# SwiGLU of a decoder block on one Trainium2 core: first products of four weight blocks in a row, scalings moved to VectorE, weight sums later

## The chip, the core and the metric

The kernel runs on one core of a Trainium2 chip. TensorE multiplies, VectorE, ScalarE and GpSimd work on tiles of 128 partitions, and SyncE (SP) issues most of the DMAs. The metric is the device time of one execution in microseconds (us).

## What is computed

A decoder block with one layer: three mixing branches, their gated sum projected and added to `h`, then a SwiGLU, and a last norm. The change lies in the SwiGLU and in what leads into it:

```python
D_MODEL = 1024; SEQ = 1024; N_META = 16; D_FF = 2816

h = h + m @ w_o
hn = rms_norm(h, norm2_g)
gate, up = jnp.split(hn @ w_gate_up, 2, axis=-1)
return h + (jax.nn.silu(gate) * up) @ w_down
# afterwards: rms_norm(h, final_g)[:, N_META:]
```

## The kernel before

Activations lie transposed: features on the partitions, the 1024 tokens along the rows of a tile, in two halves of 512. Full precision is kept by splitting every operand into a high half (fp32r, a cast on ScalarE) and a low half (the rest, a subtraction on VectorE or GpSimd). A product of two operands is three matmuls a slice, high x high, high x low, low x high, in `gemm` (lines 268 to 270). A "product" below is four slices of 128 features with 512 tokens, 12 matmuls.

The projection `w_gate_up` is worked off in 22 blocks of 128 output columns. A block is a 2x2 product: the weights are A11, A12 (the two halves of the gate's 1024 input features) and A21, A22 (the same of the up part); the normed `h` is B11, B21 (first 512 tokens, first and second 512 features) and B12, B22 (the other 512 tokens). It is done with Strassen-Winograd, seven products instead of eight: A11 B11, A12 B21, S1 T1, S4 B22, S2 T2, S3 T3 and A22 T4. S1 to S4 are sums of weights, made on GpSimd for each block (`pair_sums`, lines 1909 to 1912; S1, S2, S4, S3 in this order); T1 to T4 are sums of the B's, made once. `keys` names the B's and T's in the order of the numbers 0 to 6 that `ORDERS` uses. The down projection that follows works in the same manner, in three groups.

Block 0 is written apart in `mlp`: four direct products on B11 and B21 (gate and up), then four on T1 and B22 that add up two and two in PSUM. Blocks 1 to 21 run over `plans` and `steps`: `ahead` makes weight factors (`factor`: cast on ScalarE, low half on VectorE) four products ahead, `gemm` multiplies, and `consume` adds the results up one product later, makes the SiLU, and `put` multiplies gate and up on GpSimd.

The tiles `y{half}{o}` hold `h` for a half of the tokens and eight feature tiles `o`. The first half is normed and split while the output projection runs (`out_proj`, `first`). For the second half `stat(1)` sums squares with TensorE during the first product, `bcast(1)` spreads the factors by TensorE and a ScalarE copy (line 1662), and `sum_t1` scales: tiles 4 to 7 by their gain on ScalarE (`prescale`, line 1717) and by the norm on GpSimd (`scaled_late`, line 1721), tiles 0 to 3 in one instruction on VectorE (`scaled`, line 1712), with T1 (line 1882) behind each. T2 and T4 are made on VectorE (lines 1956, 1957), T3 on GpSimd (line 1955). Low halves have line 295 (`sub_lo`) on every engine, casts of weights line 1782, of the B's and T's line 1796; `halves` puts off each low half until the next cast, and `settle` issues what is left.

Weights come through the tile `raw`: 512 KB for the gate or the up part of a block, two buffers, so a load can only be issued when everything that reads the part two before it is done. SP issues the loads (line 213) in program order. All engines work their queues in the order of the program text; no scheduler moves anything.

Of the kernel before, what the change touches and what calls it, by code (L numbers as in the profile page):

```python
# [123 lines left out]
class Trunk:  # L124
    SLACK = 1500.0

    def __init__(self, tc, a):
# [2175 lines left out]
```

## Time and profile before

| | us |
|---|---|
| median of 3 runs (1750.38 to 1752.44) | 1750.57 |
| the profiled execution | 1750.45 |
| its span, first to last instruction | 1748.7 |
| TensorE busy | 1667.2 (95%) |
| VectorE busy | 1344.6 (77%) |
| ScalarE busy | 763.0 (44%) |
| GpSimd busy | 881.0 (50%) |

Line numbers are those of the kernel before. Times in the views count from the start of the span. `x`, `in<-` and the like read "output <- inputs". An entry in brackets is the time that the engine stood idle before the instruction, and what released it. The stretch of interest begins near 1043 us, where the first product of the SwiGLU starts, and ends near 1105 us, where blocks 0 and 1 are done; the 140 products of the other 20 blocks follow in an unbroken pattern.

### The profile page before, as it was taken

Reading aid. Unit: us, or ns where it says so; the run is one execution under the profiler, and the core shown is the slowest. Engines: PE = TensorE matmul, PEld = TensorE weight load, DVE = VectorE, ACT = ScalarE, POOL = GpSimd, SP = SyncE. Lnnn points to the kernel's source line nnn. Section 1 sums busy time; section 2 is a strip of 40 time slices with the busy share of each in tenths; the row PEclk is TensorE's granted clock in tenths of the full one; section 3 lists DMA queues with packets and bytes.
Section 4 is the critical chain, followed back from the end, with each engine's and each line's share of the span. In section 5 each row is a group of like instructions: output and inputs, shape, how many; then the busy total and the mean of one; then the engine's idle time right before and its main releaser. Section 6 shows DMA issues by size and latency. Waiting matters only on the chain.

```text
span 1748.7 us, 22588 instructions
## 1 busy us (share of the span) xinstructions
PE 1667.2 (95%) x7912; PEld 1383.0 (79%) x7912; DVE 1344.6 (77%) x2100; ACT 763.0 (44%) x1439; POOL 881.0 (50%) x639
## 2 busy tenths in 40 slices
PE   6989999998999999999999998999999999898986
PEld 5778878886888887888778876788888888686866
DVE  7999996588888744888886248777777777979697
ACT  4566217456544444876622234323322324443343
POOL 4322325315555665211174136766666665697664
PEclk9989999999999999999999998999999999999998
DMA  4111123233323333310285431332333226453423
GB/s 148 49 37 33 40 85 108 69 127 101 115 97 112 118 109 119 89 53 1 85 286 184 160 102 38 109 115 91 102 103 126 93 95 233 152 199 121 145 97 115
DMA packets 91922, 190.65 MB, mean 109 GB/s; under 512 B 9552, under 2 KB 21840, under 8 KB 91808
## 3 DMA queue, kind: packets, MB, share of 16 engines
q1 hardware_dynamic: 88704, 184.13, 31.7%
q10 hardware_dynamic: 2992, 4.75, 0.7%
q8 instruction: 62, 1.02, 0.2%
q0 software_dynamic: 112, 0.33, 0.1%
q14 instruction: 52, 0.43, 0.1%
HBM read 135.43 MB, written 53.74 MB: 108 GB/s over the span
## 4 chain that ended last, share of the span: by engine, by line
PE 62%; DVE 7%; DMA 2%; issue 2%; ACT 1%; POOL 1%; DVEq 0%; ACTq 0%; SPq 0%; POOLq 0%
PE ps L268 18%; PE ps L270 18%; PE ps L269 18%; PE ps L1446 2%; DMA y<-T 1%; DVE y L295 1%; PE ps L1422 1%; PE ps L1423 1%; PE ps L1421 1%; PE ps L1470 1%; PE ps L1471 1%; PE ps L1472 1%; DVE y L1712 1%; DVE h L1825 1%; DMA s<-y 1%
## 5 line engine op out<-in xcount | busy, mean ns | idle before, releaser
L268 PE MATMUL ps<-xh,whi 128*128 128x512 f32 (+1 forms) x492 | 175.0, 356 | 4.7 <-DVE u L863 2.4
L270 PE MATMUL ps<-xh,wlo 128*128 128x512 f32 (+1 forms) x492 | 173.9, 354 | 1.1 <-DVE wlo L239 1.1
L269 PE MATMUL ps<-xl,whi 128*128 128x512 f32 (+1 forms) x492 | 174.0, 354 | 0.6 <-POOL xl L295 0.4
L1825 DVE TENSOR_TENSOR c<-c,ps 128x512 f32<-128x512 f32 x175 | 119.4, 682 | 54.3 <-PE ps L270 49.6
L1847 POOL TENSOR_TENSOR h<-c,c 128x512 f32<-128x512 f32 x44 | 68.9, 1585 | 120.8 <-issue 75.1
L1834 ACT ACTIVATE c<-c 128x512 f32<-128x512 f32 x44 | 27.8, 632 | 207.5 <-DVE c L1825 207.5
L268 PEld LDWEIGHTS ps<-xh,whi 128*128 128x128 f32 x492 | 93.6, 190 | 17.8 <-DVE u L863 2.7
L270 PEld LDWEIGHTS ps<-xh,wlo 128*128 128x128 f32 x492 | 93.7, 190 | 14.9 <-DVE wlo L239 1.9
L269 PEld LDWEIGHTS ps<-xl,whi 128*128 128x128 f32 x492 | 93.7, 191 | 13.3 <-POOL xl L295 1.3
L239 POOL TENSOR_TENSOR wlo<-raw,whi 128x1024 fp32r<-128x1024 f32 x21 | 51.7, 2461 | 98.9 <-ACT whi L233 98.9
L269 PE MATMUL ps<-l,whi 128*128 128x512 f32 x232 | 90.9, 392 | 1.3 <-DVE l L295 1.2
L268 PE MATMUL ps<-h,whi 128*128 128x512 f32 x232 | 91.0, 392 | 0.0
L270 PE MATMUL ps<-h,wlo 128*128 128x512 f32 x232 | 90.6, 391 | 0.0
L720 DVE TENSOR_SCALAR_CACHE_REDUCE B<-sc,s 128x912 bf16<-128x912 f32 (+2 forms) x93 | 89.0, 957 | 0.1
L295 DVE TENSOR_TENSOR wlo<-sw,wlo 128x512 fp32r<-128x512 f32 (+1 forms) x49 | 57.1, 1165 | 22.7 <-ACT wlo L1782 19.5
L295 DVE TENSOR_TENSOR op<-raw,op 128x512 fp32r<-128x512 f32 (+1 forms) x42 | 56.3, 1352 | 17.0 <-ACT op L1047 17.0
L295 DVE TENSOR_TENSOR whi<-sw,whi 128x512 fp32r<-128x512 f32 (+1 forms) x50 | 50.6, 1013 | 24.4 <-ACT whi L1782 21.5
L295 DVE TENSOR_TENSOR op<-sw,op 128x512 fp32r<-128x512 f32 (+1 forms) x48 | 52.0, 1088 | 20.1 <-ACT op L1782 19.5
L295 DVE TENSOR_TENSOR whi<-raw,whi 128x512 fp32r<-128x512 f32 (+1 forms) x40 | 53.2, 1331 | 14.2 <-ACT whi L1047 12.7
L2010 POOL TENSOR_TENSOR h<-h,c 128x512 f32<-128x512 f32 x27 | 43.8, 1636 | 31.3 <-DVE c L1825 23.7
L1132 ACT COPY c<-ps 128x512 f32<-128x512 f32 x52 | 30.4, 585 | 63.8 <-PE ps L270 63.7
L1453 POOL CAST pm<-pm 16x512 fp32r<-16x512 f32 x14 | 8.5, 604 | 97.2 <-ACT pm L1449 97.2
(615 smaller groups left out, 5710.8 us busy)
## 6 DMA issues: line engine op xcount, KB each, us to landing
raw<-in_wts_dram SPq DMA_DIRECT2D x136, 512.0 KB, 3.9
T<-h SPq DMA_DIRECT2D x44, 256.0 KB, 5.3
B<-h SPq DMA_DIRECT2D x33, 256.0 KB, 2.0
y<-T SPq DMA_DIRECT2D x33, 256.0 KB, 5.7
y<-b SPq DMA_DIRECT2D x32, 256.0 KB, 2.2
s<-y SPq DMA_DIRECT2D x32, 256.0 KB, 4.9
ga<-c SPq DMA_DIRECT2D x16, 256.0 KB, 3.9
gb<-c SPq DMA_DIRECT2D x16, 256.0 KB, 4.1
```

Of the source, the lines that this page charges most:

```text
L239: e.tensor_tensor(l[:, c], r[:, c], h[:, c].bitcast(F32), op=ALU.subtract)
L268: nc.tensor.matmul(ps[:, :n], wh, xh, start=(start and k == 0), stop=False, **kw)
L269: nc.tensor.matmul(ps[:, :n], wh, xl, start=False, stop=False, **kw)
L270: nc.tensor.matmul(ps[:, :n], wl, xh, start=False, stop=(stop and k == last), **kw)
L295: getattr(self.nc, eng).tensor_tensor(lo, x, hi.bitcast(F32), op=ALU.subtract)
L720: nc.vector.tensor_scalar(junk2[:, :nk_of(i)], self.sc[i], value, None, op0=ALU.is_ge, op1=ALU.add, accum_out=at(cs, i))
L1132: nc.scalar.copy(t, ps)
L1446: nc.tensor.transpose(p3[:rows, h, :], d["S"][h][:, col:col + rows], self.ident)
L1825: nc.vector.tensor_tensor(dst, a, b, op=ALU.add)
L1834: nc.scalar.activation(t, t, AF.Silu)
L1847: nc.gpsimd.tensor_tensor(t, u, s, op=ALU.mult)
L2010: nc.gpsimd.tensor_tensor(a, a, b, op=ALU.add)
```

## The change

For blocks 0 to 3 (`NFIRST`) the two products on the first token half, A11 B11 and A12 B21, come first, eight products in a row (`first`); their results wait in tiles. So only the gate parts are loaded at first, and they are loaded a second time (`regu`) with the up parts, when these blocks run the other five products (`ORDERS[0]`). Block 0 thereby takes seven products as the others do. `prescale` and `scaled_late` go: all eight tiles of the second half are scaled by one VectorE instruction each. T1, B22, T2, T3 and T4 are made piecewise at slices of these products. The weight sums of block 0 are made behind block 3's first product, and its S4 behind block 3's second.

```diff
-ORDERS = ((0, 1, 2, 3, 4, 5, 6), (0, 1, 6, 2, 3, 4, 5), (0, 2, 3, 4, 5))
+ORDERS = ((2, 3, 4, 5, 6), (0, 1, 6, 2, 3, 4, 5), (0, 2, 3, 4, 5))
+NFIRST = 4
...
+    for f in range(NFIRST):
+        units.append(("gu", f * P, KT))
     for f in range(NFF):
-        units.append(("gu", f * P, KT))
+        units.append(("gu" if f >= NFIRST else "regu", f * P, KT))
         units.append(("gu", DFF + f * P, KT))
...
-        def prescale(o):
-            h2 = self.y[o, 1]
-            nc.scalar.activation(h2, h2, AF.Copy, scale=self.cols["g2"][:, o:o + 1])
-
-        def scaled_late(o, eng="gpsimd"):
-            h2 = self.y[o, 1]
-            getattr(nc, eng).tensor_tensor(h2, h2, rbs[1], op=ALU.mult)
-            return h2
...
-        A.append(self.factor(g[:, 512:], "gpsimd"))
+        A.append(self.factor(first_gates[0][:, 512:], "gpsimd"))
+        self.fetch(self.n_get + 2)
         block(w7, 7, 1)
-        A += [self.factor(x, "gpsimd") for x in (u[:, :512], u[:, 512:])]
+        A += [self.factor(first_gates[1][:, q * 512:(q + 1) * 512], "vector") for q in range(2)]
         self.fetch(self.n_get + 3)
...
+    def first_gate(self, f):
+        self.fetch(self.n_get + f)
+        return self.raw.pop(self.n_get + f)
...
-        p1 = self.gemm(A11, X["B11"], 512, {3: stat1})
-        p1s = copied(p1)
-
-        def sum_t1():
-            self.bcast(1)
-            for k in range(4):
-                self.prescale(4 + k)
-            for k in range(4):
-                self.scaled_late(4 + k)
-            for k in range(4):
-                b12 = self.scaled(k, 1)
-                t1 = y[k, 0]
-                nc.vector.tensor_tensor(t1, b12, t1, op=ALU.subtract)
-                self.halves("T1", t1)
-            self.settle()
-
-        p2 = self.gemm(A12, X["B21"], 512, {2: sum_t1})
-        s0 = silu(added(p1s, p2))
-        q1 = self.gemm(A21, X["B11"], 512)
-        q1s = copied(q1)
-        q2 = self.gemm(A22, X["B21"], 512)
-        u0 = added(q1s, q2)
...
+        def first(f, x, at=None):
+            ps = self.gemm(self.A0.pop(0), X[keys[x]], 512, at)
+            if x == 0:
+                p1 = kept(f, 0)
+                self.later.append(lambda: nc.scalar.copy(p1, ps))
+                pre[f] = [p1]
+            else:
+                s0 = kept(f, 1)
+                pre[f].append(s0)
+                self.later.append(lambda: silu(added(pre[f][0], ps, s0)))
+
+        first(0, 0)
+        first(0, 1, {0: stat1})
+        g2 = self.first_gate(2)
+        self.A0 += [self.factor(g2[:, q * 512:(q + 1) * 512]) for q in range(2)]
+        first(1, 0, {1: lambda: self.bcast(1), 2: lambda: sum_t1(0), 3: lambda: sum_t1(1)})
+        self.fetch(self.n_get + NFIRST)
+        first(1, 1, {0: lambda: sum_t1(2), 2: lambda: sum_t1(3)})
         for k in range(4):
-            self.halves("B22", y[4 + k, 1])
-        self.settle()
+            self.scaled(4 + k, 1)
...
+        g3 = self.first_gate(3)
+        self.A0.append(self.factor(g3[:, :512]))
+        first(2, 0)
+        self.A0.append(self.factor(g3[:, 512:]))
+        self.n_get += NFIRST
+        self.fetch(self.n_get + 1)
+        first(2, 1, {0: lambda: late(0), 2: lambda: late(1)})
...
+            def s1():
+                start()
+                pair_sums()
+                self.fetch(self.n_get + 2 * j + 2)
+                made.append(self.factor(box["s"][0]))
...
-        ahead(4)
-        v1 = self.gemm(A11, X["T1"], 512, stop=False)
-        v2 = self.gemm(A21, X["T1"], 512, stop=False)
...
+        first(3, 0, {0: lambda: late(2), 2: lambda: late(3)})
         self.settle()
-        ahead(5)
-        for k in range(4):
-            self.halves("T3", b12[k], "gpsimd" if k % 2 else "vector")
+        ahead(1)
+        first(3, 1, {k: lambda k=k: sum_t2(k) for k in range(4)})
         self.settle()
-        box = {}
-        self.gemm(A12, X["B22"], 512, ps=v1, start=False)
-        ahead(6)
-        for k in range(4):
-            self.halves("T4", t4[k], "gpsimd" if k % 2 else "vector")
-        self.settle()
-        self.later.append(lambda: box.update(s1=silu(added(p1s, v1))))
-        self.gemm(A22, X["B22"], 512, ps=v2, start=False)
...
+        ahead(2)
+        extra = deque([{k: lambda k=k: more("T3", b12, k) for k in range(4)},
+                       {k: lambda k=k: more("T4", t4, k) for k in range(4)}, {0: self.settle}])
...
         for j, (g, o) in enumerate(steps):
...
                 at = {}
+                if extra:
+                    at = extra.popleft()
```

Three places show what the queues look like. The first is VectorE behind the norm's factors (`rst`) of the second token half; `y10` to `y17` are that half, `rb1` its factors, and `raw_1910` and `raw_1916` are gates 2 and 3 in the kernel after, and `whi`, `wlo` and `op` are tiles for weight operands, used in turn. Before:

```order
L598 SCALAR_TENSOR_TENSOR rst_1996_9889<-rst_1996_9889 128x4
L1712 SCALAR_TENSOR_TENSOR y10_1817_9213<-y10_1817_9213,cols_33_115,rb1_2000_9910 128x512
L1882 TENSOR_TENSOR y00_1813_9181<-y10_1817_9213,y00_1813_9181 128x512
L1712 SCALAR_TENSOR_TENSOR y11_1828_9284<-y11_1828_9284,cols_33_115,rb1_2000_9910 128x512
L1882 TENSOR_TENSOR y01_1824_9251<-y11_1828_9284,y01_1824_9251 128x512
L295 TENSOR_TENSOR T1l0_2003_9928<-y00_1813_9181,T1h0_2002_9927 128x512
```

After:

```order
L601 SCALAR_TENSOR_TENSOR rst_1998_9894<-rst_1998_9894 128x4
L298 TENSOR_TENSOR whi_2001_9917<-raw_1910_9746,whi_2001_9917 128x512
L298 TENSOR_TENSOR wlo_2002_9920<-raw_1910_9746,wlo_2002_9920 128x512
L1822 TENSOR_TENSOR c_2000_9916<-c_1995_9883,ps_1996_9884 128x512
L1715 SCALAR_TENSOR_TENSOR y10_1817_9213<-y10_1817_9213,cols_33_115,rb1_2004_9927 128x512
L1871 TENSOR_TENSOR y00_1813_9181<-y10_1817_9213,y00_1813_9181 128x512
```

and, behind T1's last low half, after:

```order
L298 TENSOR_TENSOR T1l3_2016_9976<-y03_1846_9395,T1h3_2015_9975 128x512
L1715 SCALAR_TENSOR_TENSOR y14_1861_9500<-y14_1861_9500,cols_33_115,rb1_2004_9927 128x512
L1715 SCALAR_TENSOR_TENSOR y15_1885_9656<-y15_1885_9656,cols_33_115,rb1_2004_9927 128x512
L1715 SCALAR_TENSOR_TENSOR y16_1903_9726<-y16_1903_9726,cols_33_115,rb1_2004_9927 128x512
L1715 SCALAR_TENSOR_TENSOR y17_1912_9773<-y17_1912_9773,cols_33_115,rb1_2004_9927 128x512
L298 TENSOR_TENSOR whi_2018_9995<-raw_1916_9784,whi_2018_9995 128x512
L1822 TENSOR_TENSOR c_2017_9986<-c_2010_9956,ps_2012_9959 128x512
L298 TENSOR_TENSOR wlo_2021_10014<-raw_1916_9784,wlo_2021_10014 128x512
```

Two low halves of gate 2 and an addition now stand ahead of T1, and four scalings between T1 and the low halves of gate 3; before, T1 came at once.

The second is ScalarE around T2's casts. `sw_2025` is block 1's S4 in the kernel before, `sw_2037` block 0's S4 in the kernel after. Before:

```order
L1782 CAST whi_2030_10020<-sw_2023_10004 128x512
L1782 CAST wlo_2031_10023<-sw_2025_10006 128x512
L1796 CAST T2h0_2034_10055<-y00_1813_9181 128x512
L1796 CAST T2h1_2036_10061<-y01_1824_9251 128x512
L1796 CAST T2h2_2038_10068<-y02_1835_9323 128x512
L1796 CAST T2h3_2040_10075<-y03_1846_9395 128x512
L1782 CAST op_2042_10080<-sw_2024_10005 128x512
```

After:

```order
L1775 CAST op_2040_10076<-sw_2035_10066 128x512
L1789 CAST T2h0_2042_10083<-y00_1813_9181 128x512
L1789 CAST T2h1_2044_10092<-y01_1824_9251 128x512
L1886 COPY h05_2034_10064<-ps_2029_10041 128x512
L1789 CAST T2h2_2046_10103<-y02_1835_9323 128x512
L1789 CAST T2h3_2048_10113<-y03_1846_9395 128x512
L1775 CAST op_2051_10122<-sw_2037_10068 128x512
```

S4's cast stood ahead of the four casts of T2 and now stands behind them, next to S1's cast ahead of them.

The third is GpSimd around the low halves of T3 and T4; `raw_2064` is block 1's up part in the kernel after, and `h` tiles are products of gate and up. Before:

```order
L1955 TENSOR_TENSOR y10_1817_9213<-y14_1861_9500,y10_1817_9213 128x512
L1955 TENSOR_TENSOR y11_1828_9284<-y15_1885_9656,y11_1828_9284 128x512
L1955 TENSOR_TENSOR y12_1839_9356<-y16_1903_9726,y12_1839_9356 128x512
L1955 TENSOR_TENSOR y13_1850_9428<-y17_1911_9771,y13_1850_9428 128x512
L295 TENSOR_TENSOR y01_2046_10087<-y11_1828_9284,T3h1_2045_10086 128x512
L295 TENSOR_TENSOR y03_2050_10095<-y13_1850_9428,T3h3_2049_10094 128x512
L295 TENSOR_TENSOR y11_2055_10118<-y05_1868_9539,T4h1_2054_10117 128x512
L295 TENSOR_TENSOR y13_2059_10126<-y07_1879_9611,T4h3_2058_10125 128x512
L1847 TENSOR_TENSOR h03_2062_10156<-c_2014_9986,c_2010_9955 128x512
L1847 TENSOR_TENSOR h13_2064_10160<-c_2063_10158,c_2060_10136 128x512
```

After:

```order
L1977 TENSOR_TENSOR y10_1817_9213<-y14_1861_9500,y10_1817_9213 128x512
L1977 TENSOR_TENSOR y11_1828_9284<-y15_1885_9656,y11_1828_9284 128x512
L1977 TENSOR_TENSOR y12_1839_9356<-y16_1903_9726,y12_1839_9356 128x512
L1977 TENSOR_TENSOR y13_1850_9428<-y17_1912_9773,y13_1850_9428 128x512
L298 TENSOR_TENSOR y01_2058_10139<-y11_1828_9284,T3h1_2057_10138 128x512
L298 TENSOR_TENSOR y03_2062_10155<-y13_1850_9428,T3h3_2061_10154 128x512
L298 TENSOR_TENSOR y11_2069_10175<-y05_1868_9539,T4h1_2068_10174 128x512
L1925 TENSOR_TENSOR sw_2074_10195<-raw_2064_10164 128x512
L1926 TENSOR_TENSOR sw_2075_10196<-sw_2074_10195,raw_2039_10074 128x512
L1927 TENSOR_TENSOR sw_2076_10197<-raw_2039_10074,sw_2075_10196 128x512
L1928 TENSOR_TENSOR sw_2077_10198<-raw_2039_10074,raw_2064_10164 128x512
L298 TENSOR_TENSOR y13_2073_10189<-y07_1879_9611,T4h3_2072_10188 128x512
```

The four weight sums of the next block now stand between the two low halves of T4.

## Rows read from the trace of the kernel before

**Rows 1.** The page, part 1: busy us (share of the span), instructions

```profile
PE 1667.2 (95%) x7912; PEld 1383.0 (79%) x7912; DVE 1344.6 (77%) x2100; ACT 763.0 (44%) x1439; POOL 881.0 (50%) x639
```

**Rows 2.** TensorE waiting, 1035 to 1130 us: total us, times, longest

```profile
PE ps L269 <- DVE T1l L295: 8.7, 3, 4.1
PE ps L268 <- ACT whi L1782: 1.3, 1, 1.3
```

**Rows 3.** TensorE in time: start, us, operation [idle before, what ended it]

```profile
1050.10 0.77 PE L268 MATMUL ps<-B11h,oq 128*128 128x512 f32 x1
...
1052.80 0.47 PE L268 MATMUL ps<-B21h,oq 128*128 128x512 f32 x1
...
1072.63 0.80 PE L269 MATMUL ps<-T1l,oq 128*128 128x512 f32 x1 [3.38 <-DVE T1l L295]
...
1075.34 0.63 PE L268 MATMUL ps<-T1h,op 128*128 128x512 f32 x1
...
1076.62 0.51 PE L268 MATMUL ps<-T1h,op 128*128 128x512 f32 x1
...
1084.25 0.39 PE L268 MATMUL ps<-B11h,whi 128*128 128x512 f32 x1
...
1086.97 0.39 PE L268 MATMUL ps<-B21h,wlo 128*128 128x512 f32 x1
...
1102.05 0.50 PE L268 MATMUL ps<-T4h,whi 128*128 128x512 f32 x1 [1.31 <-ACT whi L1782]
```

**Rows 4.** VectorE in order of time

```profile
1054.93 0.75 DVE L1712 SCALAR_TENSOR_TENSOR y<-y,cols,rb 128x512 f32<-128x512 f32 x1 [1.43 <-ACT rb L1662]
1055.71 1.73 DVE L1882 TENSOR_TENSOR y<-y,y 128x512 f32<-128x512 f32 x1
...
1074.19 0.68 DVE L1825 TENSOR_TENSOR c<-c,ps 128x512 f32<-128x512 f32 x1
...
1081.46 0.68 DVE L1956 TENSOR_TENSOR y<-y,y 128x512 f32<-128x512 f32 x1
...
1089.17 0.69 DVE L295 TENSOR_TENSOR op<-sw,op 128x512 fp32r<-128x512 f32 x1
...
1102.02 0.69 DVE L295 TENSOR_TENSOR whi<-raw,whi 128x512 fp32r<-128x512 f32 x1 [1.20 <-ACT whi L1782]
```

**Rows 5.** GpSimd in order of time

```profile
1055.59 6.38 POOL L1721 TENSOR_TENSOR y<-y,rb 128x512 f32<-128x512 f32 x4 [2.31 <-ACT y L1717]
1061.93 1.73 POOL L1909 TENSOR_TENSOR sw<-raw 128x512 f32<-128x512 f32 x1
...
1068.65 6.75 POOL L1955 TENSOR_TENSOR y<-y,y 128x512 f32<-128x512 f32 x4
...
1106.39 1.30 POOL L1909 TENSOR_TENSOR sw<-raw 128x512 f32<-128x512 f32 x1 [5.40 <-DMA raw<-in_wts_dram]
...
1112.52 3.44 POOL L1847 TENSOR_TENSOR h<-c,c 128x512 f32<-128x512 f32 x2
...
1121.57 1.29 POOL L1911 TENSOR_TENSOR sw<-raw,sw 128x512 f32<-128x512 f32 x1
1122.82 1.30 POOL L1912 TENSOR_TENSOR sw<-raw,raw 128x512 f32<-128x512 f32 x1
```

**Rows 6.** SyncE's issues of weight loads, two stretches in order of time

```profile
1050.84 29.89 SPq L213 DMA_DIRECT2D raw<-in_wts_dram  x3
...
1102.74 0.33 SPq L213 DMA_DIRECT2D raw<-in_wts_dram  x1
```

**Rows 7.** Weight loads from 1030 to 1130 us, from issue to landing

```profile
DMA to landing us min/median/max: 3.6/3.9/4.9
```

**Rows 8.** ScalarE in order of time

```profile
1087.36 0.62 ACT L1796 CAST T2h<-y 128x512 fp32r<-128x512 f32 x1 [1.31 <-DVE y L1956]
1087.88 0.62 ACT L1782 CAST op<-sw 128x512 fp32r<-128x512 f32 x1
```

**Rows 9.** Line 1825, 1070 to 1500 us: ns min/median/max, first and last start

```profile
L1825 DVE TENSOR_TENSOR c<-c,ps x148: 671/686/690, 1074.2 to 1495.6; 128x512 f32<-128x512 f32 x148
```

More of the change, by code (lines that the diff above doesn't have):

```diff
@@ L139, in __init__ @@
                 continue
-            if kind == "again":
-                self.units.append(([(self.at["in", arg], 0, kt * P)], kt))
+            if kind in ("again", "regu"):
+                self.units.append(([(self.at["in" if kind == "again" else "gu", arg], 0, kt * P)], kt))
                 continue
@@ L1744, in out_proj @@
         block(w7, 7, 0)
-        g, u = self.gate_up(0)
+        first_gates = [self.first_gate(f) for f in range(2)]
         def early():
@@ L1862, in act_sums @@
                 keep(key, p, t)
-        A11, A12, A21, A22 = self.A0
+        pre, box = {}, {}
         def stat1():
@@ L1886, in mlp, with sum_t1 @@
[L1886 to L1894 removed]
+        def sum_t1(k):
+            b12 = self.scaled(k, 1)
+            t1 = y[k, 0]
+            nc.vector.tensor_tensor(t1, b12, t1, op=ALU.subtract)
+            self.halves("T1", t1)
+            if k == 3:
+                self.settle()
@@ new lines, in late, with kept @@
+        def late(k):
+            self.halves("B22", y[4 + k, 1])
+        def kept(f, x):
+            return self.t(self.fp, [P, 512], tag=("h01", "h11", "h05", "h15")[2 * f + x - 4]) if f > 1 else ct()
+        def first(f, x, at=None):
[8 more added lines that the diff above has]
+                self.later.append(lambda: silu(added(pre[f][0], ps, s0)))
@@ L1896, in mlp @@
+        g3 = self.first_gate(3)
[5 more added lines that the diff above has]
+        first(2, 1, {0: lambda: late(0), 2: lambda: late(1)})
         thunks, made = deque(), deque()
-        plans = [(j, 512) for j in range(1, NFF)] + [(NFF + 4 * g + o, P * len(GR[g])) for g in range(len(GR)) for o in range(4)]
+        plans = [(j, 512) for j in range(NFF)] + [(NFF + 4 * g + o, P * len(GR[g])) for g in range(len(GR)) for o in range(4)]
@@ L1936, in order_of @@
         def order_of(j):
-            return ORDERS[0 if j == 1 else 2 if j >= NFF + 8 else 1]
+            return ORDERS[0 if j < NFIRST else 2 if j >= NFF + 8 else 1]
         for j, n in plans:
@@ L1958, in mlp, with more @@
             self.halves("T2", t2[k], "vector")
+        def more(key, src, k):
+            self.halves(key, src[k], "gpsimd" if k % 2 else "vector")
+        first(3, 0, {0: lambda: late(2), 2: lambda: late(3)})
         self.settle()
-        ahead(5)
-        for k in range(4):
-            self.halves("T3", b12[k], "gpsimd" if k % 2 else "vector")
+        ahead(1)
+        first(3, 1, {k: lambda k=k: sum_t2(k) for k in range(4)})
         self.settle()
-        box = {}
-        self.gemm(A12, X["B22"], 512, ps=v1, start=False)
-        ahead(6)
-        for k in range(4):
-            self.halves("T4", t4[k], "gpsimd" if k % 2 else "vector")
-        self.settle()
-        self.later.append(lambda: box.update(s1=silu(added(p1s, v1))))
-        self.gemm(A22, X["B22"], 512, ps=v2, start=False)
-        self.later.append(lambda: put(0, 0, u0, s0))
-        self.later.append(lambda: put(0, 1, added(q1s, v2), box["s1"]))
-        self.otp.release()
-        self.fp = self.pool("fin", 1)
+        ahead(2)
+        extra = deque([{k: lambda k=k: more("T3", b12, k) for k in range(4)},
+                       {k: lambda k=k: more("T4", t4, k) for k in range(4)}, {0: self.settle}])
         NP, AHEAD = 7, 4
@@ L1982, in consume @@
             b = box
+            if f < NFIRST and i == 2:
+                b["p1"], b["s0"] = pre.pop(f)
             if i == 0:
@@ L2139, in prescale @@
                 nc.scalar.activation(t, t, AF.Copy, scale=self.cols["fg"][:, o:o + 1])
-        steps = [(0, f) for f in range(1, NFF)] + [(1 + g, o) for g in range(len(GR)) for o in range(4)]
+        steps = [(0, f) for f in range(NFF)] + [(1 + g, o) for g in range(len(GR)) for o in range(4)]
         n_done = 0
@@ L2163, in mlp @@
                     loads.popleft()()
-                if n == 5 and sums:
+                if i == order_of(j)[-2] and sums:
                     sums.popleft()()
-                if n in (1, 6):
+                if n == 1 or i == order_of(j)[-1]:
                     while stores:
@@ L2250, in _layout @@
     for kind, arg, kt in unit_plan():
-        if kind == "again" or kind == "wd" and len(arg) == 3:
+        if kind in ("again", "regu") or kind == "wd" and len(arg) == 3:
             continue
```

10 lines of the change are left out of this document (7 added, 3 removed).

## The prediction

> **What bounds the kernel now.** I read the busy shares first: TensorE is busy 95% of the span [rows 1]. So a change pays where TensorE stands still, or where it has fewer products to do. The waits of TensorE around the change come next: 8.7 us in three waits for low halves of T1, and one of 1.3 us for a weight's high half [rows 2]. The row-by-row view of TensorE places them: T1 arrives in pieces until 1072.63, after a last wait of 3.38 us. A product (12 matmuls of 128x512) takes 1086.97 - 1084.25 = 2.72 us, 0.227 us a matmul. From 1075.34 to 1076.62 three matmuls take 1.28 us, 0.427 us each: that is the lower clock, and it lasted from 1072.63 to 1076.62 [rows 3]. VectorE shows why T1 is late: from 1055.71 to 1074.19 eleven instructions took 18.5 us, 1.68 us each, while GpSimd ran its scalings and sums [rows 4, 5]. With GpSimd idle, twelve instructions of the same kind took 1089.17 - 1081.46 = 7.7 us, 0.64 us each [rows 4]. Additions that read PSUM never suffer: 148 of them lie between 671 and 690 ns [rows 9].
>
> **The change, edit by edit.** One product fewer: before, block 0 needs eight (four direct ones, four on T1 and B22), now seven. That is 2.72 us [rows 3], all on TensorE. The four ScalarE scalings and the four GpSimd ones (6.38 us for four [rows 5]) go; VectorE gets four more scalings, and two low halves of weights from GpSimd. T1's chain then runs beside an idle GpSimd, at 0.64 to 0.78 us instead of 1.68. The four gate weights loaded a second time are 2 MB more on SP's queue; they cost nothing by volume, but each waits for one of only two raw buffers, and here the new waits arise. I follow them on the time axis of before.
>
> *Up to T1.* Gate 2 is loaded when GpSimd frees the buffer, at 1050.84 as now [rows 6]. A load lands 3.6 to 4.9 us after its issue [rows 7]; in the place most like these, VectorE's low half at 1102.02 frees the buffer, the issue follows at 1102.74 and GpSimd starts at 1106.39 [rows 4 to 6], 3.65 us after the issue; I take that. Gate 2 is there at 1054.5. In VectorE's and ScalarE's queues its casts stand ahead of T1: two casts, two low halves and an addition, to 1057.0. T1 is twelve instructions, four scalings at 0.78 (1054.93 to 1055.71 [rows 4]) and eight at 0.64: 8.2 us. The four other scalings take 2.8 us (0.70, between both kinds). Only then comes the low half of gate 3: ready at 1068.7. TensorE gets there earlier: the second product from 1050.10, six matmuls at the lower clock until 1052.80 [rows 3], six at the full one, 0.4 us of transposes, four products: 1065.4, plus two matmuls. First wait: 2.9 us.
>
> *S1.* The second half of gate 3 sits behind an addition and a SiLU that waits for it: its low half is ready at 1071.2 and frees the buffer for block 0's up weight. GpSimd starts on it at 1074.9, S1 is 1.3 us (alone [rows 5]), its cast 0.62 [rows 8]: 1076.9. TensorE has used up block 3's first products at 1073.7. Second wait: 3.2 us, and 1.2 us more for S1's low half, which now meets GpSimd.
>
> *S4.* ScalarE casts S4 behind all four casts of T2, so S4 waits for T2's fourth difference: ten VectorE instructions from 1076.9 (S1's low half among them). Beside them GpSimd runs four weight sums and four subtractions without a pause. These same eight took 13.5 us in before (1061.93 to 1068.65 + 6.75 [rows 5]), with VectorE at 1.68: until 1088.4. By then VectorE has done 6.8; the other 3.2 take 2.0 us: 1090.4. T2's cast and S4's give 1091.6 (0.52 between casts, 0.62 the last [rows 8]). TensorE has been idle since 1080.9. Third wait: 10.7 us. This price is the one that could be much smaller: without any delay of one engine by the other, T2 is bound by GpSimd's sixth instruction (6 x 1.25 [rows 5], 1082.4) and S4 is there at 1084.9. I take the upper end, since both ran saturated in the rows that contain these eight instructions.
>
> The Trainium skill, page "SBUF — State Buffer", section "Who interferes with whom", says that a VectorE instruction with two SBUF inputs and a GpSimd instruction that reads SBUF exclude each other for a whole instruction. By that rule a pair would take 1.29 + 0.69 = 1.98 us and S4 would come 2.0 us later (1763.2 in all); the rows have 1.68 a pair, and I keep the rows.
>
> *T4.* The last low half of T4 is on GpSimd, and the weight sums of block 1 now stand ahead of it in its queue. They need block 1's up weight, and that needs the buffer that the low half of block 0's A22 frees. From 1090.4 that is ten VectorE instructions (6.4 us), two of them beside GpSimd (1.0 more each) and 0.6 for the SiLU between: 1099.4. Then 3.65 to GpSimd's start, 6.1 for the four sums (1106.39 to 1112.52 [rows 5]; alone 5.0), 1.3 for T4: 1110.5. TensorE wants it at 1103 to 1105. Fourth wait: 6 to 7 us; block 0 ends at 1110.9.
>
> *The sum.* In before, block 1 ends at 1102.05 + 2.72 = 1104.8 and 140 products are left up to the down projection. Now 141 are left at 1110.9. After a wait as long as that TensorE runs at the lower clock for some 4 us, as from 1072.63 [rows 3]: 9.3 matmuls x 0.2 = 1.9 us. 1110.9 + 2.7 + 1.9 - 1104.8 = +10.7 us. Waits ahead of block 0's T4 need no adding: the chain (load, T1, load, T2, load, sums) sets that point, not TensorE. The profiled execution took 1750.45 us, 0.1 below the median, so the forecast is **1761.2 us**.
>
> **Rivals.** *The queues don't slow each other.* If VectorE keeps 0.64 us beside GpSimd's sums, S4 comes 6.7 us earlier, the two low halves 2.0, the sums 1.1: 9.8 of the 10.7 go, 1751.4 us. Then the kernel is not slower by anything measurable. It decides at 0.75 us an instruction or less in T2's stretch. For it: the first third of the chain does run alone. Against: every SBUF-to-SBUF instruction between 1055.71 and 1074.19.
> *The cover is long enough.* Eight first products are 21.8 us; if S1, S4 and T4 were all ready when TensorE comes, the 8.7 and 1.3 us of waits [rows 2], 1.9 of lower clock and 2.7 of product are gained and 2.9 lost: 1750.45 - 14.6 + 2.9 = 1738.7 us. That needs the buffer of gate 3 free by about 1060, eleven us before I have it; the order of VectorE's queue speaks against it, the tightness of my chain (three loads in a row) for a doubt.
> *Blocks 1 to 3 starve too.* A block of five products lasts 13.6 us and holds eight GpSimd instructions, 8 x 1.68 = 13.4. If the four sums over activations (4 x 1.3) get ahead of weight sums that TensorE waits for, 5.2 us more: 1766.4 us.
>
> **How the numbers follow.** Forecast 0.59 (1757 to 1764), no mutual slowing 0.13, cover long enough 0.18, starving 0.10. The range leaves out the 0.18 and little else: 1750 to 1767. About 0.2% (3.5 us) can be told from no change. Faster by more: 0.19. Within: 0.11, from the first rival. Slower: 0.70.
>
> **What would show it.** Right: TensorE waits for the low half of a gate near 1069, for S1 near 1074 to 1077, some 10 us for S4's cast ahead of its first product on B22, and some 6 us for GpSimd's low half of T4; T1's instructions on VectorE at 0.7 us, T2's at 1.6. Wrong: T2's instructions at 0.7, a wait for S4 under 5 us, or TensorE in block 0 without a wait over 3 us.

## The result, and the profile after

The changed kernel takes 1767.88 us (median of 4 runs, 1765.73 to 1769.78), the kernel before beside it 1751.17 us: a ratio of 1.0094, 95% interval 1.0077 to 1.0112. It is slower by 16.7 us. The forecast had the direction, but 10.7 us, and its range ended at 1767.0. The profiled execution took 1769.78 us, 19.3 more than that of before; it is the longest of the four.

The page of the kernel after, part 1, answers to [rows 1]:

```profile
PE 1677.1 (95%) x7900; PEld 1388.1 (79%) x7900; DVE 1348.1 (76%) x2112; ACT 761.2 (43%) x1437; POOL 876.1 (50%) x637
```

TensorE has 12 matmuls fewer, one product, as the change says, and is yet busy 9.9 us longer. Of these, 6.2 us lie between the first product of the SwiGLU and block 7, where more matmuls ran at the lower clock: they start 0.43 us apart there and not 0.23. The other 3.7 are spread over the stretches ahead of it and behind it. Its waits, 1035 to 1180 us (total, times, longest), against [rows 2]:

```profile
PE ps L271 <- ACT op L1775: 11.6, 2, 8.5
PE ps L272 <- POOL y L298: 6.0, 1, 6.0
PE ps L273 <- DVE whi L298: 1.6, 1, 1.6
PE ps L271 <- ACT wlo L1775: 1.6, 1, 1.6
...
PE ps L273 <- DVE wlo L298: 0.5, 1, 0.5
```

The 8.7 us for T1 are gone, and 21.3 us for weights and for T4 stand in their place. In order of time (TensorE; start, us, operation, in brackets the idle time before and what ended it), against [rows 3]:

```profile
1071.57 0.50 PE L273 MATMUL ps<-B11h,whi 128*128 128x512 f32 x1 [1.64 <-DVE whi L298]
...
1079.99 0.79 PE L271 MATMUL ps<-T1h,op 128*128 128x512 f32 x1 [3.10 <-ACT op L1775]
...
1094.38 0.80 PE L271 MATMUL ps<-B22h,op 128*128 128x512 f32 x1 [8.53 <-ACT op L1775]
...
1113.74 0.80 PE L272 MATMUL ps<-y,whi 128*128 128x512 f32 x1 [6.02 <-POOL y L298]
...
1114.77 0.63 PE L271 MATMUL ps<-T1h,wlo 128*128 128x512 f32 x1
...
1119.87 0.40 PE L271 MATMUL ps<-B22h,op 128*128 128x512 f32 x1
...
1146.20 0.50 PE L271 MATMUL ps<-T1h,wlo 128*128 128x512 f32 x1 [1.63 <-ACT wlo L1775]
...
1147.45 0.79 PE L273 MATMUL ps<-T1h,wlo 128*128 128x512 f32 x1 [0.52 <-DVE wlo L298]
...
1150.59 0.39 PE L271 MATMUL ps<-T1h,wlo 128*128 128x512 f32 x1
...
1219.66 0.39 PE L271 MATMUL ps<-B11h,wlo 128*128 128x512 f32 x1
```

The four waits that the forecast named are there, in its order: gate 3's low half, S1, S4, T4's last low half. Block 0 ends at 1114.77. Then twelve matmuls take 5.10 us to 1119.87, 0.425 each, the lower clock. A fifth wait, which the forecast did not have, stands at block 3's S1 (1146.20, 1147.45), again with the lower clock behind it, until 1150.59. The last row is the start of block 7. In the kernel before, these are the end of block 1 and the start of block 7 (TensorE):

```profile
1105.18 0.39 PE L268 MATMUL ps<-B11h,wlo 128*128 128x512 f32 x1
...
1200.38 0.39 PE L268 MATMUL ps<-B11h,whi 128*128 128x512 f32 x1
```

So 35 products took 95.2 us before, 2.72 each. After, 36 products (15 of blocks 1 to 3, 21 of blocks 4 to 6) took 1219.66 - 1114.77 = 104.9 us, 7.0 more than 36 x 2.72. The whole loss lies ahead of block 7: 1219.66 - 1200.38 = 19.28.

VectorE beside GpSimd in the kernel after, VectorE first, against [rows 4]:

```profile
1059.89 0.75 DVE L1715 SCALAR_TENSOR_TENSOR y<-y,cols,rb 128x512 f32<-128x512 f32 x1 [0.66 <-ACT rb L1665]
1060.67 0.69 DVE L1871 TENSOR_TENSOR y<-y,y 128x512 f32<-128x512 f32 x1
...
1084.46 1.76 DVE L1978 TENSOR_TENSOR y<-y,y 128x512 f32<-128x512 f32 x1
1086.26 1.64 DVE L1979 TENSOR_TENSOR y<-y,y 128x512 f32<-128x512 f32 x1
...
1091.27 0.69 DVE L1979 TENSOR_TENSOR y<-y,y 128x512 f32<-128x512 f32 x1
...
1095.01 0.69 DVE L298 TENSOR_TENSOR op<-sw,op 128x512 fp32r<-128x512 f32 x1
```

GpSimd, against [rows 5]:

```profile
1078.03 1.26 POOL L1925 TENSOR_TENSOR sw<-raw 128x512 f32<-128x512 f32 x1 [24.98 <-DMA raw<-in_wts_dram]
...
1083.96 6.73 POOL L1977 TENSOR_TENSOR y<-y,y 128x512 f32<-128x512 f32 x4
...
1106.48 1.30 POOL L1925 TENSOR_TENSOR sw<-raw 128x512 f32<-128x512 f32 x1 [2.54 <-DMA raw<-in_wts_dram]
...
1111.97 1.72 POOL L298 TENSOR_TENSOR y<-y,T4h 128x512 fp32r<-128x512 f32 x1
...
1126.16 1.29 POOL L1925 TENSOR_TENSOR sw<-raw 128x512 f32<-128x512 f32 x1 [4.90 <-DMA raw<-in_wts_dram]
...
1144.24 1.26 POOL L1925 TENSOR_TENSOR sw<-raw 128x512 f32<-128x512 f32 x1 [3.20 <-DMA raw<-in_wts_dram]
...
1162.24 1.30 POOL L1925 TENSOR_TENSOR sw<-raw 128x512 f32<-128x512 f32 x1 [2.82 <-DMA raw<-in_wts_dram]
```

T1's chain runs at 0.69 to 0.75 us an instruction with GpSimd idle until 1078.03; six instructions of T2's chain take 1.64 to 1.76 while GpSimd works, and 0.69 the moment it stops (1091.27). The weight sums of blocks 1 to 4 start at 1106.48, 1126.16, 1144.24 and 1162.24, each time on a load: 18 to 19.7 us apart. TensorE needs 5 x 2.72 = 13.6 us for the five products of such a block.

### The profile page after: what moved, and what is told of

Its sections match the earlier page's. It is cut to its first block, busy times and chain, and to the rows that moved or that the text cites. A ratio compares the mean times of both kernels' runs of the same rounds, so it can differ in the third digit from the quotient of the medians.

```text
span 1767.9 us, 22575 instructions
## 1 busy us (share of the span) xinstructions
PE 1677.1 (95%) x7900; PEld 1388.1 (79%) x7900; DVE 1348.1 (76%) x2112; ACT 761.2 (43%) x1437; POOL 876.1 (50%) x637
## 3 DMA queue, kind: packets, MB, share of 16 engines
q10 hardware_dynamic: 2992, 4.75, 0.7%
## 4 chain that ended last, share of the span: by engine, by line
PE 60%; DVE 8%; issue 3%; POOL 2%; DMA 2%; ACT 1%; DVEq 0%; ACTq 0%; POOLq 0%; SPq 0%
PE ps L273 17%; PE ps L271 17%; PE ps L272 17%; PE ps L1449 2%; DVE y L298 1%; PE ps L1425 1%; PE ps L1426 1%; PE ps L1473 1%; PE ps L1424 1%; PE ps L1474 1%; PE ps L1475 1%; DVE c L1822 1%; DVE y L1715 1%; DVE h L1822 1%; DVE l L298 1%
## 5 line engine op out<-in xcount | busy, mean ns | idle before, releaser
L1844 POOL TENSOR_TENSOR h<-c,c 128x512 f32<-128x512 f32 x42 | 64.8, 1563 | 117.9 <-issue 68.1
L271 PEld LDWEIGHTS ps<-xh,whi 128*128 128x128 f32 x492 | 93.4, 190 | 17.9 <-DVE u L866 2.7
L298 DVE TENSOR_TENSOR op<-sw,op 128x512 fp32r<-128x512 f32 (+1 forms) x53 | 58.3, 1104 | 26.7 <-ACT op L1775 26.3
L1925 POOL TENSOR_TENSOR sw<-raw 128x512 f32<-128x512 f32 (+1 forms) x34 | 51.2, 1505 | 40.4 <-DMA raw<-in_wts_dram 40.4
L272 PE MATMUL ps<-y,whi 128*128 128x512 f32 x130 | 51.8, 398 | 6.9 <-POOL y L298 6.0
```

The costliest lines, as they stand in the source:

```text
L271: nc.tensor.matmul(ps[:, :n], wh, xh, start=(start and k == 0), stop=False, **kw)
L272: nc.tensor.matmul(ps[:, :n], wh, xl, start=False, stop=False, **kw)
L298: getattr(self.nc, eng).tensor_tensor(lo, x, hi.bitcast(F32), op=ALU.subtract)
L1844: nc.gpsimd.tensor_tensor(t, u, s, op=ALU.mult)
L1925: e.tensor_tensor(s1, u[:, :n], u[:, n:2 * n], op=ALU.add)
```

## Experiments

### What sets the pace of blocks 1 to 3

Theory A: block 0's end and the pace behind it are set by chains of loads and queues, so a wait that is taken away comes back later. Theory B: each wait is a price of its own. Run t4 takes the 6.02 us away:

```diff
-                       {k: lambda k=k: more("T4", t4, k) for k in range(4)}, {0: self.settle}])
+                       {k: lambda k=k: more("T4", t4, k) if k < 3 else (more("T4", t4, k), self.settle())
+                        for k in range(4)}])
```

> The changed kernel, with one edit: the last low half of T4 is issued one product earlier, so that on GpSimd it stands ahead of the weight sums of block 1 (in the changed kernel it stood behind them, and TensorE waited 6.0 us for it, after which 5.7 us ran at the lower clock). Theory A (from block 0 on the pace is set by a loop of 18 to 20 us a block, in which each up weight's load waits for a buffer, and TensorE needs 13.6 us for a block's five products): the 6.0 us go from T4 and come back as waits at the S1 products of blocks 1 to 3; the time falls by 0 to 3 us, to 1765 to 1768. Theory B (each wait is a price of its own): 6.0 us and the 2.7 us of the lower clock go, to about 1759.

Measured: 1765.81 us, ratio to before 1.0080 (1.0065 to 1.0095), 2.1 us below the changed kernel; four runs each can't tell that difference from none, but it rules out theory B's 1759. The wait at T4 is gone, and TensorE waits at the S1 of every one of blocks 1 to 3 (TensorE in t4, blocks 1 and 2):

```profile
1108.66 0.50 PE L271 MATMUL ps<-T1h,wlo 128*128 128x512 f32 x1 [0.32 <-ACT wlo L1775]
...
1126.53 0.50 PE L271 MATMUL ps<-T1h,whi 128*128 128x512 f32 x1 [1.73 <-ACT whi L1775]
```

The S1 products are 17.9 us apart, though the five products from one to the next need only 13.6. What fills the 18 us is on GpSimd, ScalarE and VectorE. ScalarE in t4:

```profile
1107.99 0.62 ACT L1775 CAST wlo<-sw 128x512 fp32r<-128x512 f32 x1 [4.45 <-POOL sw L1925]
1111.04 0.62 ACT L1775 CAST op<-sw 128x512 fp32r<-128x512 f32 x1 [2.43 <-POOL sw L1927]
1114.89 0.63 ACT L1831 ACTIVATE c<-c 128x512 f32<-128x512 f32 x1 [3.23 <-DVE c L1822]
...
1116.45 0.62 ACT L1775 CAST wlo<-raw 128x512 fp32r<-128x512 f32 x1
```

VectorE in t4:

```profile
1111.69 1.12 DVE L298 TENSOR_TENSOR op<-sw,op 128x512 fp32r<-128x512 f32 x1 [1.83 <-ACT op L1775]
1112.73 2.12 DVE L1822 TENSOR_TENSOR c<-c,ps 128x512 f32<-128x512 f32 x3
...
1119.19 1.19 DVE L298 TENSOR_TENSOR wlo<-raw,wlo 128x512 fp32r<-128x512 f32 x1
```

GpSimd in t4, the first sum of the next block:

```profile
1124.56 1.26 POOL L1925 TENSOR_TENSOR sw<-raw 128x512 f32<-128x512 f32 x1 [3.04 <-DMA raw<-in_wts_dram]
```

GpSimd's sum for block 1 starts at 1106.66, S1's cast at 1107.99, S4's cast, behind S4's sum, at 1111.04. S4's low half stands on VectorE until 1112.8, and three additions for the block before stand behind it in VectorE's queue until 1114.85. The last product that they read, S2 T2 of block 0, had ended by 1103, so they waited for their turn and not for TensorE. ScalarE waits 3.23 us for them, to make the SiLU, and A22's cast, the last cast that reads the up weight, comes behind the SiLU at 1116.45. A22's low half, behind three more additions on VectorE, ends at 1120.4, and only then can the next up weight be loaded: GpSimd starts on it at 1124.56. That is the loop of 18 us. Run ord is t4 with A22's product third, so that its cast and low half come two products earlier:

```diff
-ORDERS = ((2, 3, 4, 5, 6), (0, 1, 6, 2, 3, 4, 5), (0, 2, 3, 4, 5))
+ORDERS = ((2, 3, 6, 4, 5), (0, 1, 6, 2, 3, 4, 5), (0, 2, 3, 4, 5))
```

> As t4, and the products of blocks 0 to 3 in the order S1, S2, A22 B22, T2 or S4, so that A22's low half is cast two products earlier and the up weight's buffer comes free earlier. Theory A (the loop of load, sums, casts and buffer sets the pace): the loop falls below the 13.6 us that TensorE needs for a block, the waits of blocks 1 to 3 go, and the time falls by 8 to 12 us against the changed kernel, to 1756 to 1760. Theory B (each wait is a price of its own): like t4, about 1759, and no more than 2 us from t4 either way.

What the expectations of ord and s4 call S2 is S4: ord's order is S1 T1, S4 B22, A22 T4, S2 T2, S3 T3.

Measured: 1761.80 us, 1.0057 (1.0041 to 1.0072), 4.0 below t4. From 1106 to 1148 us TensorE in ord has no idle time (stretch, its length; busy us and instructions of TensorE's matmuls, its weight loads, VectorE, ScalarE, GpSimd; granted clock; DMA share, GB/s):

```profile
1106.00:1120.00 14.00, 14.00 (x59) 11.44 (x58) 8.43 (x11) 2.81 (x5) 7.05 (x6) 0.92 0.24 81
1120.00:1134.00 14.00, 14.00 (x63) 11.62 (x62) 8.87 (x11) 3.43 (x6) 7.26 (x6) 1.00 0.31 107
1134.00:1148.00 14.00, 14.00 (x63) 11.59 (x62) 8.79 (x10) 5.09 (x9) 11.35 (x9) 1.00 0.49 166
```

The waits of blocks 1 to 3 went with the shortened loop, so the loop caused them, as theory A has it. It did not fall below 13.6 us, as A expected: the weight sums of blocks 1 to 3 start at 1103.07, 1118.91 and 1134.06, 15.8 and 15.2 us apart. TensorE's S1 products, 13.6 us apart, live on the lead of the sums, which shrinks from 9.9 us at block 1 to 6.1 at block 3. The gain against the changed kernel is 6.1 us and not A's 8 to 12; waits of 1.58 and 2.03 us for T4, which is now wanted one product after S4, stay.

### What makes S4 late

> The changed kernel, with one edit: the factor S2 of block 0 (second in its order of products, the operand that the 8.5 us wait was for) is cast before VectorE's chain for T2 and not behind it. The factor is then there on time, and the wait, if T2 or T3 is behind it anyway, moves to the product that reads T2 or T3. Theory A: the 8.5 us become 4 to 8 us at the next product, since T2's chain ends no earlier (it ends 1.2 us later by the one cast that goes ahead); time within 3 us of the changed kernel. Theory B: the 8.5 us go wholly, to about 1759.

```diff
+        ahead(2)
         first(3, 1, {k: lambda k=k: sum_t2(k) for k in range(4)})
         self.settle()
-        ahead(2)
```

Run s4: 1767.54 us, 1.0086 (1.0069 to 1.0103), no change against the changed kernel. S4's wait is gone, and the next product waits 6.52 us for S2's cast, behind T2's (TensorE in s4):

```profile
1094.49 0.79 PE L271 MATMUL ps<-T2h,whi 128*128 128x512 f32 x1 [6.52 <-ACT whi L1775]
```

So it was T2's chain, not the place of one cast. Is the chain long because of GpSimd? Run subs moves GpSimd's four subtractions for T3 to where it stands idle:

```diff
         for k in range(4):
             self.scaled(4 + k, 1)
+            nc.gpsimd.tensor_tensor(y[k, 1], y[4 + k, 1], y[k, 1], op=ALU.subtract)
...
-            nc.gpsimd.tensor_tensor(b12[k], b22[k], b12[k], op=ALU.subtract)
```

> The changed kernel, with one edit: GpSimd's four subtractions for T3 are issued right behind the scalings of the second half's upper blocks, where GpSimd stands idle, and no longer beside VectorE's chain for T2. If VectorE's 1.65 to 1.76 us an instruction in that chain (0.69 to 0.75 us in T1's) come from GpSimd working beside it, four of GpSimd's eight operations less there bring S4's low half 3 to 5 us earlier: the 8.5 us wait falls to 4 to 6 us. By the theory that the loop of loads sets the end (A), the time falls by 0 to 3 us, since the later waits grow; by the theory that each wait is its own price (B) it falls by 3 to 5 us, to about 1764. If the chain's length has another cause, the 8.5 us stay.

Measured: 1764.47 us, 1.0076 (1.0058 to 1.0094), 3.4 below the changed kernel. VectorE in subs:

```profile
1067.76 4.75 DVE L1715 SCALAR_TENSOR_TENSOR y<-y,cols,rb 128x512 f32<-128x512 f32 x4
1072.44 1.75 DVE L298 TENSOR_TENSOR whi<-raw,whi 128x512 fp32r<-128x512 f32 x1
...
1085.56 1.66 DVE L1979 TENSOR_TENSOR y<-y,y 128x512 f32<-128x512 f32 x1
1087.15 0.68 DVE L1978 TENSOR_TENSOR y<-y,y 128x512 f32<-128x512 f32 x1
```

T2's chain runs at 0.68 once GpSimd's sums are done. But the four scalings grew from 2.73 to 4.75 us and gate 3's low half from 0.69 to 1.75: the price moved with the work. Gate 3 waits 4.73 us, S1 1.19 + 0.52, S4 6.46 (not 4 to 6).

Run g3 instead brings the load forward: both casts of gate 3 into the middle of T1's chain, and the up weight's fetch behind them.

```diff
+        g3 = self.first_gate(3)
+        self.A0 += [self.factor(g3[:, q * 512:(q + 1) * 512]) for q in range(2)]
+        self.n_get += NFIRST
+        self.fetch(self.n_get + 1)
         first(1, 1, {0: lambda: sum_t1(2), 2: lambda: sum_t1(3)})
...
-        g3 = self.first_gate(3)
-        self.A0.append(self.factor(g3[:, :512]))
...
-        self.A0.append(self.factor(g3[:, 512:]))
-        self.n_get += NFIRST
-        self.fetch(self.n_get + 1)
```

> The changed kernel, with one edit: both casts and low halves of gate 3 stand in the middle of T1's chain and no longer behind it and behind the scalings of the second half, and block 0's up weight is fetched right behind them. Its raw buffer comes free some 8 us earlier, so block 0's weight sums start on GpSimd near 1069 and not at 1078. Theory A (a chain of loads and of VectorE's queue sets block 0's end, TensorE only fills it): the waits for gate 3 (1.6 us) and S1 (3.1 us) go, the wait for S4 keeps 5 to 9 us because VectorE's queue behind T1 is as long as before, and the chain as a whole moves up by 4 to 8 us: about 1760 to 1764. Theory B (each wait is its own price): 4.7 us go, 1763. Rival C: VectorE's own work sets T2, whatever the load does; then GpSimd's sums slow VectorE earlier, S4 comes less than 2 us earlier and the time stays at 1766 to 1768.

Measured: 1764.05 us, 1.0073 (1.0056 to 1.0090), 3.8 below the changed kernel. GpSimd starts at 1066.43, as meant, and meets the scalings, which take 6.78 us for four; S1's cast stands in ScalarE's queue behind B22's, which wait for VectorE (TensorE in g3):

```profile
1081.88 0.80 PE L271 MATMUL ps<-T1h,op 128*128 128x512 f32 x1 [11.83 <-ACT op L1775]
```

Counted from the first product of the SwiGLU, the sums start 9.2 us earlier, but S4's low half ends only 2.3 us earlier (48.4 us, against 50.7 in the changed kernel). The time is one that A and B expected; what the queues show is mostly rival C's mechanism, VectorE setting T2 whatever the load does. With ord's edits:

> The edits of the runs named ord and g3 together. If the early chain and the loop of blocks 1 to 3 are two separate limits, their gains add up: 6 us of ord and 4 to 8 us of g3, 1754 to 1758. If the early chain only hands its time to the waits behind it, no more than 2 us below ord, about 1760.

Measured: 1758.22 us, 1.0036 (1.0024 to 1.0048): 3.6 below ord, 9.7 below the changed kernel, by the medians about the sum of the two gains (6.1 and 3.8). So block 0's chain and the loop behind it are two limits. Run vord settles VectorE's part; it is ord with block 0's sums and T3's subtractions on VectorE:

```diff
-                e = nc.gpsimd
+                e = nc.vector if j == 0 else nc.gpsimd
...
-            nc.gpsimd.tensor_tensor(b12[k], b22[k], b12[k], op=ALU.subtract)
+            nc.vector.tensor_tensor(b12[k], b22[k], b12[k], op=ALU.subtract)
```

> As ord, and block 0's weight sums and the four subtractions for T3 run on VectorE, so that GpSimd does nothing beside T2's chain. VectorE has 8 instructions of 0.65 us more (5.2 us) ahead of S4's low half, and six instructions of 1.65 to 1.77 us become 0.65 to 0.7. If mutual slowing is the cause, the chain from S1's low half to S4's falls from 15.8 us to 11 to 13, every instruction in it takes 0.7 us, and S4's wait falls from 10.6 to 7 to 8 us: about 1758 to 1759. If T2's instructions were long for another reason, they stay at 1.7 us and the time grows by 5 us.

Measured: 1757.46 us, 1.0041 (1.0026 to 1.0056), 4.3 below ord by the medians, 2.8 by the ratios. The 22 instructions of VectorE from the sums to S4's low half start 0.60 to 0.79 us apart, the chain from the start of S1's low half to the end of S4's falls from 15.8 to 11.6 us, and S4's wait from 10.62 to 4.86. With eight instructions more VectorE is done earlier. VectorE in vord, one of T2's differences:

```profile
1080.36 0.68 DVE L1978 TENSOR_TENSOR y<-y,y 128x512 f32<-128x512 f32 x1
```

By time alone four runs each do not tell t4, subs and g3 from the changed kernel, whose own four span 4.0 us. The profiles order them alike: counted from the first product of the SwiGLU, block 4 begins at 117.6 us in the changed kernel, at 117.4 in s4, 116.0 in t4, 114.6 in subs, 113.2 in g3, 110.4 in ord, 108.2 in g3ord and 107.4 in vord. By this count g3ord has 9.4 of the 11.5 us that g3 and ord gain apart.

### The change's second part alone, and a better kernel

Runs scal and scallate put the change's scalings (and, in scallate, the later weight sums) into the kernel before.

```diff
-            for k in range(4):
-                self.prescale(4 + k)
-            for k in range(4):
-                self.scaled_late(4 + k)
...
             self.settle()
+            for k in range(4):
+                self.scaled(4 + k, 1)
```

> The kernel before, with one part of the change: the second half's upper tiles are scaled by one VectorE instruction each, behind T1, and not on ScalarE and GpSimd. Then only the weight sums of block 1 stand in GpSimd's queue beside T1's chain. If GpSimd's work is what makes T1's instructions 1.68 us long, four sums beside the chain cost it some 4 us where eight operations cost it 10: T1's waits fall from 8.7 us to 2 to 5 us, the time to 1746 to 1749. If the lower clock or another cause made them long, 1751.

> As scal, and GpSimd's four subtractions for T3 stand ahead of block 1's weight sums, so that these come later and GpSimd has nothing to do beside T1's chain (the change's third idea without its first). If mutual slowing is the cause, T1 ends near 1063 and its 8.7 us of waits go but for 0 to 2 us, with the lower clock behind them (1.9 us); the low halves of B22, now beside GpSimd, may cost 1 to 3 us: 1741 to 1746. If block 1's sums are then late for S1 of block 1, the gain goes there, and the time is 1748 to 1751.

Measured: 1750.94 us, 0.9994 (0.9984 to 1.0003), and 1751.38 us, 0.9996 (0.9987 to 1.0006): no change, against gains of 2 to 10 us expected from mutual slowing. The times are those that the expectations gave for other causes, but the traces don't show these: T1's waits fell as mutual slowing has it, to 3.7 us in scal and to nothing in scallate, and S1 of block 1 has no wait. Other waits stand in their place (TensorE in scallate; the last row is the start of block 2):

```profile
1073.01 0.80 PE L268 MATMUL ps<-B22h,oq 128*128 128x512 f32 x1 [3.49 <-ACT B22h L1796]
...
1102.82 0.50 PE L268 MATMUL ps<-T4h,whi 128*128 128x512 f32 x1 [3.06 <-ACT whi L1782]
...
1107.54 0.40 PE L268 MATMUL ps<-B11h,wlo 128*128 128x512 f32 x1
```

The second of them cost twice. The product behind it took 4.72 us at a mean granted clock of 0.64 (4.71 and 0.64 in scal), against 3.13 us at 1.00 in before, where the wait was 1.31. Counted from the first product of the SwiGLU, that product starts 2.1 us earlier than before in scal and 2.0 earlier in scallate, but block 2 only 0.6 and 0.4.

B22's cast stands behind block 0's first SiLU, and that behind VectorE's scalings beside GpSimd (4.78 us for four). Run b22 moves B22 ahead of the SiLU:

```diff
             for k in range(4):
                 self.scaled(4 + k, 1)
+                self.halves("B22", y[4 + k, 1])
+            self.settle()
```

> As scal, and the casts and low halves of B22 stand right behind each scaling of the second half's upper tiles, ahead of block 0's first addition and SiLU on VectorE and ScalarE (in scal and scallate TensorE waited 2.0 and 3.5 us for a cast of B22 that stood behind that SiLU in ScalarE's queue). If that queue position is what ate the gain, the wait for B22 falls to 0 to 1 us, TensorE reaches block 1's last product 2 to 3 us earlier, and waits there (2.8 us in scal) up to 3 us more, since VectorE's queue for T2 to T4 is as full as before: 1748 to 1751, no more than 3 us below the kernel before. If each wait were its own price: 2.3 us and the lower clock behind it go, 1747.

Measured: 1753.36 us, 1.0015 (1.0006 to 1.0024): a miss, a little slower. The cast's wait is gone, but B22's low halves wait 1.8 us (each scaling and low half now meets one of GpSimd's subtractions) and block 1's last product 3.9, after which it takes 5.29 us at a granted clock of 0.50. VectorE finishes T4's low halves 55.1 us behind the first product in b22 as in before, 53.0 and 53.1 in scal and scallate. That VectorE's queue bounds b22 is what this suggests. Run vec tests it: b22 with GpSimd all but emptied, block 1's sums, T3's subtractions and all low halves of T3 and T4 on VectorE, the sums behind the gate's two factors and no longer ahead of them.

```diff
-                e = nc.gpsimd
+                e = nc.vector if j == 1 else nc.gpsimd
...
-            self.halves("T3", b12[k], "gpsimd" if k % 2 else "vector")
+            self.halves("T3", b12[k], "vector")
...
-            self.halves("T4", t4[k], "gpsimd" if k % 2 else "vector")
+            self.halves("T4", t4[k], "vector")
...
+            def two():
+                pair_sums()
+                self.fetch(self.n_get + 2 * j + 2)
+                sum_(0)
```

> The kernel before with GpSimd taken out of the stretch: the scalings of the second half, block 1's weight sums, the subtractions for T3 and all low halves of T3 and T4 run on VectorE, and B22's casts and low halves stand as in b22. VectorE gets 12 instructions of 0.65 us (7.8 us) more than in b22, and loses the lengthening of about 11 instructions by 1.0 to 1.1 us each that scal's trace shows. If an instruction beside GpSimd really costs VectorE about 1 us, the waits of T1 (8.7 us in before) and B22 stay away, T4 is done 7 to 10 us earlier than before, and the time is 1741 to 1746. If it only moves VectorE's work about, VectorE is the bound and the time is 1747 to 1752.

Measured: 1748.16 us, 0.9976 (0.9967 to 0.9986): in the range expected for VectorE as the bound, 1747 to 1752, and not in 1741 to 1746. No wait for T1 or B22 is left; T4's low halves are done 51.5 us behind the first product, 3.7 earlier than before, not 7 to 10. Two waits remain, both for casts on ScalarE (TensorE in vec):

```profile
1088.07 0.80 PE L268 MATMUL ps<-T2h,op 128*128 128x512 f32 x1 [3.52 <-ACT op L1782]
...
1098.55 0.50 PE L268 MATMUL ps<-T4h,whi 128*128 128x512 f32 x1 [1.74 <-ACT whi L1782]
```

Run vec2 moves these two casts up (S2's ahead of T2's chain, A22's ahead of T4's casts):

```diff
+        ahead(5)
         for k in range(4):
             nc.vector.tensor_tensor(b12[k], b22[k], b12[k], op=ALU.subtract)
...
-        ahead(5)
...
-        ahead(6)
+        ahead(7)
```

> As vec, with two casts moved up in ScalarE's and VectorE's queues: S2's factor of block 1 stands ahead of T2's chain (in vec TensorE waited 3.5 us for its cast behind all four casts of T2), and A22's factor of block 1 ahead of T4's casts (1.7 us of wait behind a SiLU). If these are only queue positions in front of TensorE, both waits go but for 1 to 2 us at T2's last low halves: 2 to 4 us below vec, 1744 to 1746. If VectorE's total work is the bound that the waits only mark, the 3.5 us move to T2's low halves and the time stays within 1 us of vec, 1747 to 1749.

Measured: 1745.15 us, 0.9964 (0.9950 to 0.9977), 3.0 below vec: the fastest kernel here, 6.7 us below the kernel before and 22.7 below the changed one. VectorE finishes T4's low halves no earlier than in vec (51.9 us behind the first product), yet block 2 starts 2.0 us earlier: what was left in vec were places in ScalarE's queue, as expected. TensorE's waits around T2 to T4 in vec2 (1035 to 1180 us):

```profile
PE ps L269 <- DVE y L295: 2.3, 2, 1.6
...
PE ps L268 <- ACT op L1782: 0.5, 1, 0.5
```

## Why the forecast had the direction and not the size

**T1 alone on VectorE: right.** 0.69 to 0.75 us an instruction, as forecast.

**The four waits: right in place and order.** 1.64 us for gate 3 (forecast 2.9), 3.10 for S1 (3.2, and 1.2 more for its low half, which came without a wait), 8.53 for S4 (10.7), 6.02 for T4 (6 to 7). T2's chain beside GpSimd took 1.64 to 1.76 us an instruction (forecast 1.68); subs and vord show that GpSimd's work is the reason. The rival that the queues don't slow each other falls.

**Block 0's end: 1.7 us too small.** Forecast 6.1 us behind block 1's end in before (1110.9 - 1104.8). Measured 1114.77 - 1105.18 = 9.6; of these 1.8 lie ahead of the SwiGLU, whose first product starts at 1044.98 here and at 1043.22 in before. The other 7.8 are this step. (The forecast point itself was 2.1 early; the forecast also had block 1's end in before 0.4 early, at 1104.8 and not 1105.18, and took that off.) The miss built up in the loads and queues of the chain: with the 1.8 taken off, T1's chain starts 1.1 us later than the 1057.0 forecast, GpSimd 1.4 later than 1074.9, block 1's sums 1.7 later than 1103.05 (1099.4 + 3.65).

**One product more to do: right**, 2.72 us.

**The lower clock: 1.9 us forecast, 2.4 measured** behind T4 (12 matmuls x (0.425 - 0.227)).

**"141 products unbroken": this step failed.** The forecast laid the remaining products end to end behind block 0. They were broken: 36 products took 7.0 us more than 36 x 2.72, 2.4 of it the lower clock above; block 3's waits (1.63 + 0.52) and the lower clock until 1150.59 (7 matmuls in 3.14 us, 1.6 too long) are 3.7, and 0.9 is spread. So 4.6 us were missing here. It was not the rival "blocks 1 to 3 starve too" as written either: its number (1766.4) is close, but its cause, sums over activations ahead of weight sums on GpSimd, is not what happened: the weight sums of blocks 1 to 4 each waited for a load. The forecast followed the loop of load, sums, casts and buffer once, from block 0 to block 1, and did not ask for its period. One pass took 18 us, against 13.6 of TensorE's work; t4 and ord show it. The wait for T4 in block 0 hid this at first, since it let the sums run ahead: only block 3's S1 had to wait.

Together: 7.8 + 2.7 + 2.4 + 4.6 = 17.5 us, against 16.7 between the medians; the 1.8 ahead of the SwiGLU make it 19.3, what lies between the two profiled executions. The forecast's 10.7 lacks 6.8 of the 17.5: 4.6 by the failed step, 1.7 by block 0's end, 0.5 by the clock.

**The rival "cover is long enough"** fell with the first three waits.

**VectorE beside GpSimd.** By the Trainium skill, page "SBUF — State Buffer", section "Who interferes with whom", a VectorE instruction with two SBUF inputs and a GpSimd instruction that reads SBUF exclude each other. In the changed kernel a pair takes 1.68 us (four subtractions in 6.73 us, beside four VectorE instructions), not 0.69 + 1.29 = 1.98: the trace agrees on who is slowed, not on the full price. The same section of the Trainium skill says that a VectorE instruction with at most one SBUF input, outside the two-port modes, does not contend with GpSimd. The trace agrees: in g3 an addition that reads PSUM took 0.67 us at 1074.89 in the middle of GpSimd's subtractions, and the four scalings ahead of it, which read two tiles in SBUF, 1.7 each.

## What to carry to other kernels

When work is brought forward to cover a late operand, follow the new order's buffers over one whole period, from load to load of the same buffer, and compare that with the work that the busy engine has for it: the first block's waits show only the first turn. A period that is a little too long can be lived with for a few blocks, as in ord, out of the lead that the first block leaves. Beside a saturated VectorE, an SBUF-to-SBUF instruction on GpSimd cost VectorE about 1.0 us here where doing it itself costs 0.65; where VectorE's queue sets the end, take such work back. A wait that goes away counts only if the next late operand doesn't stand in the same queue.
